# First output projection as seven half products, with all B, C and x projections ahead of the scans

## The chip, the cores and the metric

The kernel runs on one core of a Trainium2 chip. A core has five engines that run side by side, each with its own queue of instructions: TensorE (PE; its weight loads are listed as PEld), VectorE (DVE), ScalarE (ACT), GpSimd (POOL) and SyncE (SP), which issues most transfers. The metric is the device time of one execution in microseconds. A profile is taken of one execution.

## The reference

One inference step of a small trunk of two layers with width 1024. There are 1024 prompt tokens and 8 sequences of 8 new tokens, together 1088 token columns (`TOK`). Each layer is `x = x + (1 + gate) * mixer(rmsnorm(x) * (1 + scale) + shift)`, where shift, scale and gate come from a conditioning vector.

- Layer 1 is a Mamba-2 SSD mixer. One projection gives a gate z (2048 wide), x (2048), B and C (8 groups of 128 each) and dt (32 heads). x, B and C go through a causal convolution of four taps and a Silu. Then comes a scan over chunks of 128 tokens, for 8 groups of 4 heads each, with a state for each head that goes from chunk to chunk; the 64 sample tokens start from given states. The result is multiplied by silu(z), normalised over each group, and projected from 2048 back to 1024 (the output projection).
- Layer 2 is a pooling mixer: projections u and z, window means of u over 2, 4, 8 and 16 tokens, a product inside each of 4 groups, a gate, and a second output projection.
- A last norm gives y. The new convolution, scan and pool states are outputs too.

All is in fp32. Most matrix products are written as three matmuls on split numbers: a high part (fp32r) and the rest, hi*hi + hi*lo + lo*hi. Small products in the scan use plain fp32.

## The kernel before, in words

Activations lie with channels on the 128 partitions and tokens along the free axis. A tile is 128 channels by 1088 tokens. SBUF tiles of that size come from a set of 30 slots (`Slots`, 7 wide ones more in the second half). The program is written in one order, and a scheduler at build time places each instruction in its engine's queue: an instruction that is ready early may go ahead of one written before it. On the chip the queues are then in order.

Two ways of making a pair of projection tiles exist. The plain way (`mm1`, `mm3`, L179 to L187) takes three token chunks of 368, 368 and 352 (`CH`), and for each of 8 input blocks three matmuls. The fast way (`fast_run`, L1010) is a Strassen-like scheme over a pair of tiles: seven products of half the size (4 input blocks, 544 tokens as two quarters of 272), with sums of activations (`act_sums_front`, L1420, once) and of weights (`w_sums`, L939, for each pair: GpSimd makes four sums, and `split_half`, L167, splits seven half tiles into high and low parts).

Layer 1 runs like this:

- `front` (L1353) makes the norm, the first four gate tiles the plain way and dt. `front_pairs` (L1461) then makes twelve pairs the fast way, listed in `FRONT`: gates z for groups 2 to 7, and B, C and x for groups 5, 7 and 0. B, C and x tiles go through the convolution (`conv_tile`, L335), and those of groups 5 and 7 are stored in DRAM (`xbd`).
- `ssd_layer` (L1517) runs the eight scans. `scan_group` (L506) is a generator that stops after each chunk; after each stop, `FILL` says how many units of other work are written in. Those units come from `beside` (L1553): the plain projections of B, C and x for groups 1, 2, 3, 4 and 6 (one unit is one token chunk of one tile, 24 matmuls), with the blocks that make shift, scale and gate (`ada_block`, L239) between them, and then the first output projection.
- The first output projection (`op_unit`, L761) works on four parts of 4 input tiles each (`PARTS`). For each of the 8 output tiles it multiplies one part, scales by the gate and adds to x. Parts 0 to 2 are beside the scans; between the parts x goes to DRAM and back. The last part (`last_part`, L785) makes the squares and the norm of layer 2 with it, in three token chunks.

In a scan chunk `front` (L536) loads `acb`, a broadcast of the cumulative decay (two buffers), takes exponentials on ScalarE (L545, L558, L559), makes C*B and three transposes on TensorE, and products on VectorE (L561 to L577). `states` (L585) makes the chunk states, `rows` (L602) the output. At the group's end `back_sample` and `state_sample` (L637, L658) treat the sample tokens, with masked copies on ScalarE (L662) and matmuls on split numbers (L665).

Layer 2 starts with two pairs the plain way (`plain_pairs`, L871) and fourteen the fast way (`fast_pairs`, L1081). After the pooling products the second output projection already runs as seven half products: `ORDER` lists them, `block_steps` (L1154) makes the activation blocks, `ow_fetch`, `ow_add` and `ow_split` (L1184 to L1223) fetch, sum (by an accumulating DMA on GpSimd's queue) and split the weight blocks, `out_product` (L1252) multiplies, and `contribute` (L1225) adds each product to the places that need it.

## Time and profile before

| what | value |
|---|---|
| median of 3 runs | 1635.8 us (1634.3 to 1637.19) |
| the profiled execution's own time | 1634.35 us |
| its span, first to last instruction | 1632.6 us |
| TensorE busy | 1598.2 us, 98% |
| VectorE busy | 1170.1 us, 72% |
| ScalarE busy | 862.5 us, 53% |
| GpSimd busy | 443.0 us, 27% |
| from HBM, to HBM | 201.12 MB, 70.23 MB |

A row of the groups of instructions reads: line, engine, operation, what is written and read, shape and count, then busy time and the mean duration of one in ns, then the engine's idle time before them and what ended it. A duration holds the run through the engine's pipeline, so neighbours overlap and the distance of two starts is shorter. A row of a stretch gives start and end, length, busy time and number of instructions for each engine, the granted clock, the DMA share and GB/s. A row of a timeline gives the start in us and the duration.

From the trace, the stages of the execution: the twelve fast pairs from 95.9 to 358.6 us, the scan groups start at 358.6, 432.2, 507.4, 582.5, 657.9, 731.7, 809.0 and 879.9, the first output projection ends at 1000.3, the plain part of the pool projection at 1053.9, the fast part at 1353.8, the pool products at 1448.8.

### The profile page before, as it was taken

To read this page: it belongs to the slowest core of one execution; us is meant where nothing else is said; L and a number is where in the kernel's file an instruction comes from. 1 tells how busy PE (TensorE), PEld (TensorE's weight loads), DVE (VectorE), ACT (ScalarE), POOL (GpSimd) and SP (SyncE) were. 2 spreads that over 40 slices of the span, in tenths; PEclk is the share of its full clock that TensorE was granted. 3 is DMA by queue.
4 is the path that set the end of the run, shared out by engine and by line. 5 is a ranking of instruction groups with operands and counts; after the bars stand their busy time and mean duration, and the time that the engine had idled before them with its cause. 6 is when DMAs were issued, how large, how long until landed. Compare 5 with 4: busy or idle time off the path is not lost. (4 is left out here: it accounts for less than half of the span.)

```text
span 1632.6 us, 30674 instructions
## 1 busy us (share of the span) xinstructions
PE 1598.2 (98%) x12061; PEld 1521.7 (93%) x12061; DVE 1170.1 (72%) x1914; ACT 862.5 (53%) x1737; POOL 443.0 (27%) x525
## 2 busy tenths in 40 slices
PE   8999999999999999999999999999999999999997
PEld 6899999998889898888999899999999999999996
DVE  6873467568787888789878867955556547577886
ACT  6663454467667667675645536633434344333364
POOL 0233354411221202120212222354444530000241
PEclk9999999999999999999999999999999999999999
DMA  9422232354654554678889542133323369665783
GB/s 346 163 71 96 81 124 80 110 181 141 196 158 159 166 191 130 219 230 305 283 313 311 203 140 95 45 126 104 108 100 104 124 202 359 197 164 182 164 168 114
DMA packets 122305, 275.59 MB, mean 169 GB/s; under 512 B 18192, under 2 KB 59312, under 8 KB 122160
## 3 DMA queue, kind: packets, MB, share of 16 engines
q1 hardware_dynamic: 118128, 260.91, 46.8%
q0 software_dynamic: 4032, 12.72, 4.5%
q8 instruction: 95, 1.56, 0.4%
q14 instruction: 50, 0.41, 0.1%
HBM read 201.12 MB, written 70.23 MB: 166 GB/s over the span
## 5 line engine op out<-in xcount | busy, mean ns | idle before, releaser
L999 PE MATMUL st<-hh,w 128*128 128x272 f32 x832 | 240.4, 289 | 1.9 <-POOL w L175 1.9
L997 PE MATMUL st<-hh,w 128*128 128x272 f32 x832 | 240.2, 289 | 0.0
L998 PE MATMUL st<-hl,w 128*128 128x272 f32 x832 | 239.6, 288 | 0.0
L997 PE MATMUL st<-t,w 128*128 128x272 f32 x624 | 181.5, 291 | 3.9 <-DVE z L1027 2.1
L998 PE MATMUL st<-t,w 128*128 128x272 f32 x624 | 180.8, 290 | 0.7 <-DVE t L911 0.7
L999 PE MATMUL st<-t,w 128*128 128x272 f32 x624 | 181.1, 290 | 0.0
L181 PE MATMUL mm<-hh,wh 128*128 128x368 f32 (+1 forms) x528 | 178.1, 337 | 0.1
L183 PE MATMUL mm<-hh,wl 128*128 128x368 f32 (+1 forms) x528 | 173.4, 328 | 0.0
L182 PE MATMUL mm<-hl,wh 128*128 128x368 f32 (+1 forms) x528 | 173.3, 328 | 0.0
L999 PEld LDWEIGHTS st<-hh,w 128*128 128x128 f32 x832 | 156.5, 188 | 2.4 <-POOL w L175 2.4
L998 PEld LDWEIGHTS st<-hl,w 128*128 128x128 f32 x832 | 156.8, 188 | 0.0
L997 PEld LDWEIGHTS st<-hh,w 128*128 128x128 f32 x832 | 156.6, 188 | 0.1
L598 POOL TENSOR_TENSOR hd<-h,cd 128x256 f32<-128x256 f32 x56 | 49.4, 883 | 340.8 <-DVE h L599 185.2
L181 PE MATMUL mm<-gh,wh 128*128 128x368 f32 (+1 forms) x384 | 129.3, 338 | 1.6 <-ACT raw L420 1.5
L1249 PE MATMUL op<-b,w 128*128 128x272 f32 x448 | 128.9, 288 | 1.1 <-DVE b L1178 1.1
L1248 PE MATMUL op<-b,w 128*128 128x272 f32 x448 | 129.5, 289 | 0.0
L1250 PE MATMUL op<-b,w 128*128 128x272 f32 x448 | 129.0, 288 | 0.0
L182 PE MATMUL mm<-gl,wh 128*128 128x368 f32 (+1 forms) x384 | 125.9, 328 | 0.2 <-DVE gl L745 0.2
L183 PE MATMUL mm<-gh,wl 128*128 128x368 f32 (+1 forms) x384 | 126.0, 328 | 0.0
L997 PEld LDWEIGHTS st<-t,w 128*128 128x128 f32 x624 | 119.1, 191 | 4.8 <-DVE z L1027 2.3
L998 PEld LDWEIGHTS st<-t,w 128*128 128x128 f32 x624 | 118.6, 190 | 1.0 <-DVE t L911 0.9
L999 PEld LDWEIGHTS st<-t,w 128*128 128x128 f32 x624 | 118.7, 190 | 0.0
(300 smaller groups left out, 4432.7 us busy)
## 6 DMA issues: line engine op xcount, KB each, us to landing
wr<-win SPq DMA_DIRECT2D x48, 512.0 KB, 3.6
acb<-acd SPq DMA_DIRECT2D x64, 256.0 KB, 4.5
wr<-pin SPq DMA_DIRECT2D x32, 512.0 KB, 3.5
wr<-pout SPq DMA_DIRECT2D x28, 512.0 KB, 4.8
x<-x1d SPq DMA_DIRECT2D x24, 544.0 KB, 5.5
x1d<-x SPq DMA_DIRECT2D x22, 544.0 KB, 5.0
wr<-pout POOLq DMA_DIRECT2D x20, 512.0 KB, 6.1
x<-xT SPq DMA_DIRECT2D x16, 544.0 KB, 5.8
```

The costliest lines, as they stand in the source:

```text
L181: nc.tensor.matmul(ps[:, :n], hi[:, k, :], ah[:, a:a + n], start=first, stop=False)
L182: nc.tensor.matmul(ps[:, :n], hi[:, k, :], al[:, a:a + n], start=False, stop=False)
L183: nc.tensor.matmul(ps[:, :n], lo[:, k, :], ah[:, a:a + n], start=False, stop=last)
L598: nc.gpsimd.tensor_tensor(out=hd, in0=h[-1], in1=cd.unsqueeze(2).to_broadcast([P, 4, 64]), op=ALU.mult)
L997: nc.tensor.matmul(ps[c], hi[:, k], xh[:, t], start=(k == 0 and not more), stop=False, skip_group_check=True)
L998: nc.tensor.matmul(ps[c], hi[:, k], xl[:, t], start=False, stop=False, skip_group_check=True)
L999: nc.tensor.matmul(ps[c], lo[:, k], xh[:, t], start=False, stop=(k == 3), skip_group_check=True)
L1248: nc.tensor.matmul(ps[:, :QUART], hi[:, k], xh, start=k == 0, stop=False)
L1249: nc.tensor.matmul(ps[:, :QUART], hi[:, k], xl, start=False, stop=False)
L1250: nc.tensor.matmul(ps[:, :QUART], lo[:, k], xh, start=False, stop=k == 7)
```

## The change

- `FRONT` now lists sixteen fast pairs: B and C, then x, for groups 1 to 7 and then 0. All are convolved in one way; all but group 0 are stored in DRAM and read back at the end of the scan before theirs. The sixteen late ada blocks run in the front, with slots of their own for the weights.
- Beside the scans stand only the plain gate tiles of groups 2 to 7 (`gate_fill`), stored raw until both of a pair are made and then put through Silu, and then the first of the seven products of the output projection. `FILL` is 4 or 5 units a group, and 10 in the last.
- The first output projection uses the routine of the second: `out_init`, `block_steps`, `out_units`, with inputs read back from DRAM (`need_rows`) as slots allow (`room`, `reserve`). Product 2 is written beside the last scan with three accumulators, the other six after the scans (`ssd_out`).
- In the scan, the sample states are multiplied in plain fp32, half of their masks are made on VectorE, the sum of two squares is left to the ones-matmul, and a few small steps on ScalarE go.
- Layer change: the sample additions, squares, norm and modulation for the second half of the tokens are written behind products 4 and 7, those of the first half behind the first chunk of the pool projection, which now takes four token chunks of 272.
- The weight splits of the fast pairs that GpSimd did are on VectorE.

The core of the diff:

```diff
-FRONT = (("z", 2), ("z", 3), ("z", 4), ("b", 5), ("x", 5), ("z", 5), ("b", 7), ("x", 7), ("z", 6), ("b", 0), ("x", 0),
-         ("z", 7))
-BESIDE = (1, 2, 3, 4, 6)
-
-FILL = (((1,) * 10 + (2,),) * 4 + ((1,) * 9 + (4, 5),) + ((3, 2, 2, 2, 2, 2, 2, 2, 2, 2, 3),) * 2 + ((2, 2, 2, 1, 1, 1, 1, 1, 2, 2, 1),))
+FRONT = tuple((kind, g) for g in (1, 2, 3, 4, 5, 6, 7, 0) for kind in "bx")
+BESIDE = (2, 3, 4, 5, 6, 7)
+NSLOT_S = 1
+
+
...
-    def split_half(self, src, pool=False):
+    def split_half(self, src):
...
-        eng = self.nc.gpsimd if pool else self.nc.vector
-        eng.tensor_tensor(out=lo, in0=src, in1=hi.bitcast(F32), op=ALU.subtract)
+        self.nc.vector.tensor_tensor(out=lo, in0=src, in1=hi.bitcast(F32), op=ALU.subtract)
...
-            if src is None:
-                raws.append(self.stream_next_raw().rearrange("p a m -> p (a m)"))
-            else:
-                raws.append(self.slots.get("ada"))
-                nc.sync.dma_start(raws[hh][:, :1024].rearrange("p (a b) -> p a b", a=4), src[:, 4 * hh:4 * hh + 4, :])
+            raws.append(self.slots.get("ada"))
+            nc.sync.dma_start(raws[hh][:, :1024].rearrange("p (a b) -> p a b", a=4), src[:, 4 * hh:4 * hh + 4, :])
...
-        return self.gp.tile([P, 1115], F32, tag="raw", bufs=4, name=self.name("raw"))
+        return self.tp.tile([P, 1115], F32, tag="raw", bufs=5, name=self.name("raw"))
...
+    def gate_fill(self):
+
+
+        tiles = [(g, i) for g in BESIDE for i in range(2)]
+        steps = iter(())
+        for g, i in tiles:
             w = self.stream_next()
+            if i == 0:
+                dst = [self.slots.get("z") for _ in range(2)]
+            if (g, i) == tiles[-1]:
+                self.out_init(self.io["wout"], 0)
+                steps = self.half_steps()
                 ps = [self.mm_tile() for _ in CH]
                 for k in range(8):
                     for c in range(3):
                         self.mm1(ps[c], w, k, self.hn[k], CH[c], k == 0, k == 7)
                     self.slots.free(*self.hn[k])
+                    next(steps, None)
+                    if k in (1, 3, 4, 5, 6, 7):
+                        self.ow_step((k - 1) // 2 if k < 5 else k - 3)
                     if k < 7:
                         yield
                 for c in range(3):
+                    ins = self.raw_chunk(dst[i], c, ps[c])
+                for _ in steps:
+                    pass
+            else:
+                for c in range(3):
+                    ps = self.mm_tile()
+                    self.mm3(ps, w, self.hn, CH[c])
+                    ins = self.raw_chunk(dst[i], c, ps)
+                    if c < 2:
+                        yield
+            if i:
+                with self.tc.issue_after(ins.ins):
+                    for q in range(2):
+                        self.z_chunk(dst[q], dst[q], 0, TOK)
+                for q in range(2):
+                    self.gate_store(2 * g + q, dst[q])
+            yield
+
+    def ow_step(self, i):
+
+        if i < 3:
+            self.ow_fetch()
+        if 1 < i < 4:
...
-            ea = gp.tile([P, 4, 128], F32, tag="ea", bufs=3, name=self.name("ea"))
-            nc.scalar.activation(ea[:, :, :L], acb, AF.Exp)
+            ea = gp.tile([P, 4, 128], F32, tag="ea", bufs=3, name=self.name("ea")) if c else None
+            if c == 8:
+                nc.scalar.activation(ea[:, :, 0:8], acb[:, :, 7::8], AF.Exp)
+            elif c:
+                nc.scalar.activation(ea, acb, AF.Exp)
...
+                xm = gp.tile([64, 2, 256], F32, tag="xm", bufs=2, name=self.name("xs"))
+                seq = self.kc[:64, K_SEQ + 2 * b2:K_SEQ + 2 * b2 + 2]
+                if b2 % 2:
+                    for i in range(2):
+                        nc.scalar.activation(xm[:, i], xv, AF.Copy, scale=seq[:, i:i + 1])
+                else:
+                    nc.vector.tensor_tensor(out=xm, in0=xv.unsqueeze(1).to_broadcast([64, 2, 256]), in1=seq.unsqueeze(2).to_broadcast([64, 2, 256]), op=ALU.mult)
                 S = pp.tile([P, 512], F32, tag=("S", "y")[b2 % 2], bufs=1 + b2 % 2, name=self.name("S"))
                 for i in range(2):
-                    nc.tensor.matmul(S, Bt[i], xm.rearrange("p b n -> p (b n)"), start=(i == 0), stop=(i == 1))
+                    nc.tensor.matmul(S[:, 256 * i:256 * i + 256], Bt, xm[:, i], start=True, stop=True)
                 d = hsl[half][:, 512 * (b2 % 2):512 * (b2 % 2) + 512]
                 nc.vector.tensor_tensor(out=d, in0=d, in1=S, op=ALU.add)
...
+        for q in range(2):
+            for j in range(4):
+                mm = nc.tensor.matmul(ps[32 * j:32 * j + 32, :272], self.ones[:, :32], sq[q][:, 272 * j:272 * j + 272], start=q == 0, stop=q == 1,
+                                      tile_position=(0, 32 * j))
...
+        for c, ch in enumerate(((HALF, QUART), (HALF + QUART, QUART), (0, QUART), (QUART, QUART))):
             ps = [self.plain_tile(c) for _ in range(2)]
 
             for k in range(8):
                 for i in range(2):
                     self.mm1(ps[i], ws[i], k, self.hn[k], ch, k == 0, k == 7)
+            if c == 0:
+                self.first_half()
             for i in range(2):
...
+    def room(self):
+        sl = self.slots
+        return (sl.a or sl.b) and len(sl.a) + len(sl.b) + len(sl.e) > self.reserve
+
+    def need_rows(self, rows, idx):
+
+        for i in idx:
+            if i < 16 and rows[i] is None and i < self.nrows and self.room():
+                rows[i] = self.slots.get("row")
+                self.nc.sync.dma_start(rows[i], self.gyd[i])
+
     def block_steps(self, m, rows):
...
+        ada = [("G", 0, q) for q in range(4)] + [("A", 1, k) for k in range(8)] + [("G", 1, q) for q in range(4)]
+        self.ada_plan = {n: ada[max(n - 1, 0):n + 1] for n in range(0, 16, 2)}
+        self.ada_plan[15] = ada[15:]
...
+        self.rows, self.nrows, self.reserve = [None] * 16, 14, 0
+        self.fill = self.beside()
+        for _ in range(3):
+            next(self.fill)
         for g in range(8):
             sc = self.scan_group(g, T[g])
             for i, n in enumerate(FILL[g]):
                 next(sc)
+                self.reserve = (4, 2, 0, 0)[min(max(i - 6, 0), 3)]
                 for j in range(n):
                     next(self.fill)
-                    if i in (0, 3) and j == 0:
-                        next(rest, None)
+                if i in (0, 3):
+                    next(rest, None)
                 if i == 8 and g + 1 in self.G:
-                    T[g + 1] = [sl.get("xbc") for _ in range(4)]
+                    T[g + 1] = [sl.get("xbc", extra=g < 6 and j < 2) for j in range(4)]
                     for t, d in zip(T[g + 1], self.xbd[g + 1]):
                         nc.sync.dma_start(t, d)
             rest = sc
-        self.prep = self.op_part_load(3, self.acts[3])
...
+        for n in (2, 3):
+            for _ in range(n):
+                next(self.fill)
+            next(rest)
+        self.rows[14:], self.reserve = self.last_rows, 0
...
+    def beside(self):
+
+
+        yield from self.gate_fill()
+        yield from self.out_units(2, self.block_steps(6, self.rows))
 
     def ssd_out(self):
         nc, sl, x = self.nc, self.slots, self.x
+        h2 = slice(HALF, TOK)
+        for _ in range(2):
+            self.ow_fetch()
+        self.ow_add()
+        for _ in self.fill:
             pass
+        for m, nxt in ((6, 3), (3, 5), (5, 1), (1, 4)):
+            if m == 3:
+                self.load_x(range(4))
+            self.out_product(m, self.block_steps(nxt, self.rows))
+        for d in range(8):
+            self.sample_add(d)
+            nc.sync.dma_start(self.x1d[d][:, h2], x[d][:, h2])
         ss, rst = sl.get("ss"), sl.get("rst")
+        sl.free(self.sacct)
         self.hn = []
 
+        def square(d, a, first):
+            if first:
+                nc.scalar.activation(ss[:, a:a + HALF], x[d][:, a:a + HALF], AF.Square)
+                return
+            t = self.gp2.tile([P, HALF], F32, tag="mt2", bufs=self.nmt2, name=self.name("sq"))
+            nc.scalar.activation(t, x[d][:, a:a + HALF], AF.Square)
+            (nc.gpsimd if a or d > 3 else nc.vector).tensor_tensor(out=ss[:, a:a + HALF], in0=ss[:, a:a + HALF], in1=t, op=ALU.add)
+
+        def norm(a, more=()):
+            self.ms_log(ss, rst, a, QUART, 1.0 / 1024, more=list(more))
+            self.rstd(rst[:, a:a + QUART])
+
+        def modulate(k, a, n):
+            self.modulate(1, k, x[k], rst, self.hn[k][0], self.hn[k][1], a, n, x[k][:, a:a + n])
+
+        def behind4(d, c):
+            square(2 * d + c, HALF, d == c == 0)
+
+        def behind7(d, c):
+            i = 2 * d + c
+            if i == 0:
+                for _ in range(8):
+                    self.hn.append((sl.get("hh", F32R), sl.get("hl", F32R)))
+                with self.ln_set():
+                    norm(HALF)
+                    norm(HALF + QUART)
+            else:
+                modulate(i - 1, HALF, HALF)
+            if c == 0:
+                square(4 + d, 0, d == 0)
+            else:
+                square(d, 0, False)
+                nc.sync.dma_start(self.x1d[d][:, :HALF], x[d][:, :HALF])
+            if i == 4:
+                self.stream_init(self.pool_items)
+                self.stream_raw(0)
+                self.wsw = 1
+            if i == 5:
+                self.stream_raw(1)
+            if i == 6:
+                self.stream_split(0)
+                self.stream_split(1)
+                modulate(7, HALF, HALF)
+
+        self.out_product(4, self.block_steps(7, self.rows), behind4)
+        for d in range(4, 8):
+            nc.sync.dma_start(self.x1d[d][:, :HALF], x[d][:, :HALF])
+        self.out_product(7, iter(()), behind7)
+
+        def first_half():
+            with self.ln_set():
+                norm(0)
+                norm(QUART)
+            for a in (0, QUART):
                 for k in range(8):
+                    modulate(k, a, QUART)
+            sl.free(ss, rst)
+
+        self.first_half = first_half
 
     def pool_layer(self):
         nc, io, sl = self.nc, self.io, self.slots
...
```

515 lines of the change are left out of this document (177 added, 338 removed).

## The prediction

> **What bounds the kernel now.** I read the page's busy time first, then the busy time of each engine over stretches cut where the work changes, then the groups of instructions by shape, and TensorE's timeline for single prices.
>
> ```profile
> span 1632.6 us, 30674 instructions
> PE 1598.2 (98%) x12061; PEld 1521.7 (93%) x12061; DVE 1170.1 (72%) x1914; ACT 862.5 (53%) x1737; POOL 443.0 (27%) x525
> ```
>
> TensorE is busy for all but 34.4 us. So time is gained where matmuls go away, and lost where TensorE begins to wait. The stretches below are, in order: the fast projections (twelve pairs of tiles), the third scan group, the sixth and the eighth scan group, the plain part of the pool projection, and the fast part of it. Columns: start and end, length, then busy time and count for each engine, granted clock, DMA share, GB/s.
>
> ```profile
> core 0: us, PE busy (x) PEld busy (x) DVE busy (x) ACT busy (x) POOL busy (x), PEclk, DMA share, GB/s
> 95.90:358.60 262.70, 257.93 (x2037) 255.87 (x2036) 154.68 (x233) 129.30 (x252) 106.45 (x117) 0.99 0.30 102
> 507.40:582.50 75.10, 75.10 (x587) 67.44 (x588) 61.96 (x94) 51.39 (x117) 15.42 (x27) 1.00 0.53 168
> 731.70:809.00 77.30, 75.82 (x580) 68.38 (x579) 71.18 (x126) 47.77 (x108) 12.10 (x13) 1.00 0.87 285
> 879.90:938.00 58.10, 56.37 (x447) 51.68 (x446) 48.42 (x96) 31.75 (x80) 10.12 (x9) 1.00 0.69 239
> 1000.30:1053.90 53.60, 50.39 (x294) 47.95 (x293) 50.77 (x97) 35.15 (x82) 16.41 (x26) 1.00 0.15 46
> 1053.90:1353.80 299.90, 297.43 (x2354) 296.57 (x2353) 170.64 (x247) 123.66 (x261) 134.57 (x132) 0.99 0.37 129
> ```
>
> A scan group lasts 75 us and TensorE never waits in it, because 47 us of plain projection matmuls (two pairs of tiles, priced below) lie between the scan's own. VectorE is at 61.96 of 75.10 there, and at 71.18 of 77.30 in the sixth group, where TensorE idles 1.5 us. The reader is to see that the scans are covered by projection work, and that this cover is what the change takes away.
>
> **The change part by part.** Pace of the two kinds of matmul, from stretches that hold nothing else (fast pairs; pool mix; second output projection), and the count of the one that goes:
>
> ```profile
> 1090.00:1290.00 200.00, 200.00 (x1597) 200.00 (x1596) 117.47 (x167) 78.30 (x170) 92.24 (x94) 1.00 0.31 108
> 1360.00:1440.00 80.00, 80.00 (x486) 79.82 (x485) 55.66 (x77) 25.66 (x30) 3.47 (x4) 1.00 0.73 246
> 1450.00:1550.00 100.00, 100.00 (x802) 100.00 (x801) 74.17 (x138) 34.62 (x44) 13.68 (x18) 1.00 0.69 185
> L181 PE MATMUL mm<-gh,wh 128*128 128x368 f32 (+1 forms) x384 | 129.3, 338 | 1.6 <-ACT raw L420 1.5
> ```
>
> A 272-wide matmul costs 200/1597 = 125.2 ns in the fast pairs and 124.7 ns in the output products; a plain one (368, 368 and 352 wide) 80/486 = 164.6 ns. A fast pair is 7 x 2 x 4 x 3 = 168 matmuls, 21.03 us; a plain pair 144, 23.70 us.
>
> Projections: sixteen fast pairs instead of twelve, six plain pairs beside the scans instead of ten. Four pairs change kind: 4 x (21.03 - 23.70) = -10.7 us of TensorE.
>
> First output projection: 384 x 3 = 1152 plain matmuls, 189.6 us, become 7 x 4 x 2 x 8 x 3 = 1344 narrow ones, 167.6 us: -22.0 us.
>
> The first two pool tiles go from three chunks to four of 272: 144 matmuls (23.70) become 192 (23.94): +0.2 us.
>
> Inside the scans two things get dearer on TensorE. The sample states multiply in plain fp32 (two 256-wide matmuls, like L590) instead of two 512-wide split ones (L665), and the sum of squares is summed by eight matmuls instead of four.
>
> ```profile
> 882.48 0.40 PE L665 MATMUL S<-xs,Bt 128*128 128x512 f32 x1
> 882.71 0.40 PE L665 MATMUL S<-xs,Bl 128*128 128x512 f32 x1
> 883.50 0.67 PE L710 MATMUL ms<-z,ones 128*32 128x272 f32 x8
> 900.24 1.02 PE L590 MATMUL S<-xd,Bt 128*128 128x256 f32 x4
> 908.19 0.59 PE L590 MATMUL S<-xd,Bt 128*128 128x256 f32 x2
> L252 PE MATMUL am<-wr,scp 128*32 128x256 f32 x256 | 17.1, 385 | 0.0
> L261 PE MATMUL am<-kc,mp 128*128 128x9 f32 x96 | 12.5, 239 | 0.5 <-ACT mp L257 0.5
> ```
>
> Each fp32 matmul appears as two passes; two more passes cost 1.02 - 0.59 = 0.43 us, so two matmuls 0.86 us, against 2 x 0.23 = 0.46 us now (distance of the two starts): +0.40 us, 32 times, +12.8 us (at most +0.56 each, +18, if the drain in 1.02 is not overlapped). The second four sums repeat up to 0.67 us in each of 8 groups: +4.8 us (0 if they overlap wholly). An ada block costs 17.1/16 + 12.5/24 = 1.59 us; sixteen move from the scans to the front, 25.4 us, with no change of the sum.
>
> TensorE in all: -10.7 - 22.0 + 0.2 + 12.8 + 4.8 = -14.9 us. Less than half of the gain of the seven products is left.
>
> By stages: start 95.9 as before. Front: 262.70 - 12 x 21.03 = 10.3 stays, + 16 x 21.03 + 25.4 = 372.2. A scan group's own TensorE time is 75.10 - 2 x 23.70 - 3 x 1.59 = 22.9, with the dearer parts 22.9 + 1.6 + 0.6 = 25.1, eight of them 200.8. Gates 6 x 23.70 = 142.2, products 167.6, plain pool part 53.6 + 0.2, and 578.7 from there to the end. Sum 1611.2 us of span, with no idle time in the scans.
>
> What the other engines have to do in that time decides the rest. Their rows:
>
> ```profile
> L359 DVE SCALAR_TENSOR_TENSOR raw<-raw,cwh,raw 128x1112 f32<-128x1112 f32 x60 | 83.0, 1384 | 2.8 <-ACT raw L357 2.7
> L361 DVE SCALAR_TENSOR_TENSOR xbc<-raw,raw 128x1024 f32<-128x1024 f32 x20 | 24.4, 1221 | 14.6 <-ACT raw L360 14.5
> L139 DVE TENSOR_TENSOR wl<-wr,wh 128x1024 fp32r<-128x1024 f32 x49 | 60.9, 1243 | 12.6 <-ACT wh L138 9.6 <-PE st L999 2.6
> L564 DVE TENSOR_TENSOR xd<-tr,tkx 128x512 f32<-128x512 f32 x72 | 49.0, 680 | 0.0
> L357 ACT ACTIVATE raw<-raw,cwh 128x1112 f32<-128x1112 f32 x20 | 26.3, 1314 | 0.5
> L360 ACT ACTIVATE raw<-raw 128x1112 f32<-128x1112 f32 x20 | 22.5, 1125 | 4.1 <-DVE raw L359 4.1
> L420 ACT ACTIVATE raw<-mm 128x368 f32<-128x368 f32 x40 | 18.7, 471 | 13.6 <-PE mm L183 13.0
> L138 ACT ACTIVATE wh<-wr 128x1024 fp32r<-128x1024 f32 x49 | 51.6, 1053 | 48.2 <-PE mm L182 20.5 <-DMA wr<-win 9.6 <-issue 7.7
> L662 ACT ACTIVATE xs<-st,kc 128x256 fp32r<-128x256 f32 x64 | 27.8, 497 | 8.2 <-DVE st L655 7.2 <-PE S L665 1.0
> L300 ACT ACT_TABLE_LOAD x11 | 14.1, 1283 | 9.7 <-PE ms L710 9.6
> ```
>
> Scan group, VectorE: 61.96 less four convolutions (4 x (3 x 1.384 + 1.221) = 21.5) and four weight splits (5.0) is 35.5. After: + 1.9 for one and a half gate tiles' splits, + 2 x 0.68 for the masks it takes over, and about 2 less for the dropped split and sum: 37. ScalarE: 51.39 - 4 x (1.314 + 1.125 + 3 x 0.471 + 1.053) = 31.8; - 4 x 0.497 for the masks, + 3.7 for gate tiles, + 1.7 for their Silu (priced like L360), + 1.9 for table loads (two for each pair of tiles, 0.75 pairs a group): 37. TensorE: 25.1 and, from FILL, 30 units in seven groups, 4.3 x 3.95 = 17.0: 42.1 us. So TensorE stays the busiest, with VectorE and ScalarE at 88%. The nearest row to that mix is the eighth group, where VectorE is at 83% and TensorE idles 1.73 of 58.10, 3%. I take 3% of 367 us (the scans, the gates and the first product): +11 us. Bounds: 0, and the rate of the second rival below.
>
> Front, VectorE for one pair:
>
> ```profile
> L348 DVE SCALAR_TENSOR_TENSOR xbc<-raw,vec,xbc 128x1024 f32<-128x1024 f32 x36 | 53.0, 1472 | 9.4 <-ACT xbc L350 9.0
> L348 DVE SCALAR_TENSOR_TENSOR xbc<-raw,vec,xbc 128x64 f32<-128x64 f32 x36 | 15.3, 424 | 0.2
> L175 DVE TENSOR_TENSOR w<-sw,w 128x512 fp32r<-128x512 f32 x78 | 60.3, 775 | 35.5 <-ACT w L173 35.5
> L175 POOL TENSOR_TENSOR w<-wr,w 128x512 fp32r<-128x512 f32 x50 | 66.2, 1331 | 30.3 <-ACT w L173 30.3
> L1027 DVE TENSOR_TENSOR raw<-st,m 128x272 f32<-128x272 f32 x18 | 7.7, 436 | 4.4 <-PE st L999 4.1
> ```
>
> Two convolutions 6 x (1.472 + 0.424) = 11.4, seven splits 5.4 (those of POOL move to VectorE: 50 x 0.775 = 39 us, half of it in the pool part, where VectorE is at 170.64 of 299.90), about six sums 2.6: 19.4 us against 21.03 + 1.59 = 22.6 us of TensorE, 86%. I cost it at nothing; TensorE covers it.
>
> Products: the routine is that of the second output projection, where TensorE is at 100.00 of 100.00. New are fourteen row loads on SP's queue, fewer weight buffers in the first product, and POOL's accumulating DMAs, behind which the last group's hd waits in POOL's queue. +3 us for the handover, 0 to +12. Layer change: the two stretches around it idle 3.2 + 2.5 us. The second half's norm moves beside the last product, and the first half's stands behind one chunk (two tiles, 48 matmuls, 6 us); I take -3, from -5.7 to +6.
>
> 1611.2 + 11 + 3 - 3 = 1622.2 us of span. The profiled run takes 1634.35 us with its span of 1632.6, 1.75 around it, and the median of the runs is 1635.8, 0.1% above. Forecast: **1624 us**, 0.6% faster than the profiled run.
>
> **The rivals.** Scans no longer covered. The stretch with the least cover in the trace, four chunks of the last group with one short unit each:
>
> ```profile
> 897.70:915.70 18.00, 16.30 (x142) 15.18 (x141) 16.01 (x33) 10.17 (x33) 3.09 (x4) 1.00 0.93 319
> acb<-acd SPq DMA_DIRECT2D x64, 256.0 KB, 4.5
> ```
>
> 4.5 us a chunk with VectorE at 16.01 and TensorE idle 1.7. Eight chunks at that rate are 36. Of the 42.1 us of TensorE about 31 lie beside those chunks (three fill units, 11.9, and some 19 of the scan's own 25.1), 11 at the group's end. 36 + 11 = 47 instead of 42.1, +39 us over eight groups in place of +11: 1652 us. It decides from 3.4 us of idle a group. For it: acb has two buffers, and a load is issued only when ScalarE has read the one two chunks before, so two chunks cannot be quicker than landing and reading. Against: gate units can be drawn forward into the holes. [...]
>
> Full cover: no idle in the scans, 1611.2 - 3 + 1.75 = 1610 us. For it stands the third group's 75.10 of 75.10; against it 88% on two engines in place of 82% and 68%.
>
> VectorE bounds the front: five raw buffers hold five tiles of three pairs, so a late convolution holds back the sums that free the accumulators. One us for each pair, 1624 + 16 = 1640 us. It decides from 3.2 us over 19.4 a pair; 154.68 of 262.70 speaks against.
>
> Starved products: rows and blocks for want of slots, a few us at each of six handovers, about 1645 us.
>
> **How the numbers follow.** Forecast 0.52 (its own range 1612 to 1635, with 0.08 of it in the span of no change), full cover 0.08, uncovered scans 0.26, front bound by VectorE 0.08, starved products 0.06. About 0.2% is what a measurement of this kernel can tell from no change. Faster 0.44 + 0.08 = 0.52; same 0.08 + 0.02 = 0.10; slower 0.38. The range goes from full cover to just above uncovered scans, 1609 to 1656.
>
> **What would show it.** Right: pairs 21 us plus ada apart in the front, scan groups 42 to 44 us, TensorE busy some 15 us less in all, no idle in the products. Wrong: scan groups at 46 us or more with ScalarE or VectorE ending TensorE's waits; pairs at 24 us; TensorE's sum not lower, which would mean the fp32 states cost what the products save.

## The result, and the profile after

| | before | after |
|---|---|---|
| median, runs measured together (4 each) | 1635.05 us (1633.54 to 1637.19) | 1687.99 us (1681.16 to 1694.17) |
| profiled execution, its own time and span | 1634.35, 1632.6 us | 1681.16, 1679.4 us |
| ratio | | 1.0322, 95% interval 1.0273 to 1.0371 |

The kernel became 3.2% slower, where 0.6% faster was forecast; 1688 lies outside the range too. The profiled execution of the changed kernel took 0.4% less than the median, so what its stages lose is if anything too small.

The page of the changed kernel, span and busy time of the engines:

```profile
span 1679.4 us, 32000 instructions
PE 1616.2 (96%) x12527; PEld 1510.0 (90%) x12527; DVE 1260.4 (75%) x2072; ACT 888.2 (53%) x1727; POOL 455.6 (27%) x531
```

TensorE's busy time is up by 18 us, though its work was to shrink by 14.9 us; its idle time is up from 34 to 63 us. The stretches of the changed kernel, cut where the work changes (columns as before: start and end, length, busy time and count of each engine, granted clock, DMA share, GB/s). They are: the front's sixteen pairs, gates ahead of the scans, scan group 2 (four gate units beside it), group 4 (five units), group 7 up to product 2, product 2 with the end of group 7, product 6, product 3, product 1, product 4, the plain part of the pool projection, its fast part.

```profile
core 0: us, PE busy (x) PEld busy (x) DVE busy (x) ACT busy (x) POOL busy (x), PEclk, DMA share, GB/s
96.10:470.10 374.00, 366.99 (x3025) 353.43 (x3023) 293.90 (x454) 195.79 (x371) 116.21 (x185) 1.00 0.43 143
470.10:482.60 12.50, 12.50 (x80) 12.33 (x77) 9.06 (x15) 4.99 (x9) 1.44 (x2) 1.00 0.87 305
570.40:614.30 43.90, 42.53 (x351) 34.13 (x350) 33.68 (x60) 28.78 (x70) 11.17 (x11) 1.00 0.74 251
658.20:708.80 50.60, 48.40 (x376) 39.23 (x376) 42.40 (x71) 38.49 (x91) 12.41 (x13) 0.97 0.68 221
801.30:840.80 39.50, 35.15 (x270) 29.40 (x269) 30.33 (x56) 31.24 (x76) 5.22 (x7) 0.91 0.82 266
840.80:880.40 39.60, 36.38 (x276) 31.24 (x276) 34.11 (x56) 20.95 (x31) 7.99 (x7) 0.96 0.90 279
880.40:910.60 30.20, 25.77 (x195) 25.55 (x194) 23.35 (x38) 11.71 (x17) 1.75 (x2) 0.94 0.94 302
910.60:934.50 23.90, 23.90 (x194) 23.90 (x193) 17.38 (x36) 8.36 (x12) 3.48 (x4) 1.00 0.94 251
958.60:986.30 27.70, 25.76 (x195) 25.54 (x194) 20.08 (x38) 10.18 (x15) 11.47 (x13) 0.94 0.72 204
986.30:1021.10 34.80, 27.73 (x195) 26.33 (x194) 21.81 (x35) 18.17 (x25) 17.92 (x16) 0.90 0.74 167
1047.80:1098.00 50.20, 49.72 (x342) 48.89 (x341) 42.09 (x76) 31.52 (x71) 29.72 (x9) 1.00 0.19 65
1098.00:1397.80 299.80, 295.86 (x2355) 295.22 (x2353) 191.03 (x271) 124.61 (x262) 105.86 (x107) 1.00 0.36 129
```

Product 3 shows what a product costs undisturbed, 23.9 us; product 4 takes 34.8 with the same number of matmuls. The scan groups 0 to 6 take 39.6, 48.1, 43.9, 43.9, 50.5, 47.3 and 45.3 us, together 318.7.

Against the forecast (the allowance of 11 us for idle time in the scans is spread over them by their TensorE time):

| stage | forecast | measured | difference |
|---|---|---|---|
| up to the end of the front | 468.1 | 470.1 | +2.0 |
| gates ahead of the scans | 12.2 | 12.5 | +0.3 |
| scan groups 0 to 6 | 303.0 | 318.7 | +15.7 |
| group 7, last gate tile, product 2 | 62.7 | 79.1 | +16.4 |
| products 6, 3, 5, 1, 4, 7 | 146.6 | 167.4 | +20.8 |
| plain pool part | 50.8 | 50.2 | -0.6 |
| the rest | 578.7 | 581.4 | +2.7 |
| span | 1622.2 | 1679.4 | +57.2 |

The front, the layer change and the rest are as forecast. The loss lies between 482.6 and 1047.8 us, in three places of about the same size. TensorE's waits there (who waits, for what; total, times, longest, in us):

```profile
engine line waited for: us in total, times, longest us
PE S L604 <- ACT Bt L587: 10.9, 8, 4.1
PE op L1230 <- ACT b L1157: 5.2, 2, 4.4
PE op L1230 <- ACT w L1203: 4.7, 1, 4.7
PE op L1232 <- DVE w L1204: 4.3, 4, 1.9
PE S L679 <- ACT b L1157: 2.0, 1, 2.0
```

With the smaller ones they come to 33 us. TensorE's own terms for these stages are 498.7 us in the prediction, without idle time, and the stages take 565.2. So of 66.5 us above the terms 33 are shown as idle, and as much lies in time that is shown as busy.

### The profile page after: what moved, and what is told of

Same layout as the page of the kernel before. It is cut to its first block, busy times and chain, and to the rows that moved or that the text cites. A ratio compares the mean times of both kernels' runs of the same rounds, so it can differ in the third digit from the quotient of the medians.

```text
span 1679.4 us, 32000 instructions
## 1 busy us (share of the span) xinstructions
PE 1616.2 (96%) x12527; PEld 1510.0 (90%) x12527; DVE 1260.4 (75%) x2072; ACT 888.2 (53%) x1727; POOL 455.6 (27%) x531
## 5 line engine op out<-in xcount | busy, mean ns | idle before, releaser
L933 PE MATMUL st<-hh,w 128*128 128x272 f32 x960 | 278.9, 290 | 0.1
L935 PE MATMUL st<-hh,w 128*128 128x272 f32 x960 | 277.3, 289 | 1.0 <-DVE w L168 1.0
L1230 PE MATMUL op<-b,w 128*128 128x272 f32 x896 | 261.9, 292 | 10.0 <-ACT b L1157 5.2
L1232 PE MATMUL op<-b,w 128*128 128x272 f32 x896 | 261.3, 292 | 5.1 <-DVE w L1204 5.0
L1231 PE MATMUL op<-b,w 128*128 128x272 f32 x896 | 261.0, 291 | 2.2 <-DVE b L1158 2.1
L933 PE MATMUL st<-t,w 128*128 128x272 f32 x720 | 207.8, 289 | 5.3 <-ACT t L845 3.3
L935 PE MATMUL st<-t,w 128*128 128x272 f32 x720 | 207.4, 288 | 0.0
L934 PE MATMUL st<-t,w 128*128 128x272 f32 x720 | 207.1, 288 | 0.0
L933 PEld LDWEIGHTS st<-hh,w 128*128 128x128 f32 x960 | 180.8, 188 | 3.1 <-ACT mp L244 2.5
L1230 PEld LDWEIGHTS op<-b,w 128*128 128x128 f32 x896 | 171.7, 192 | 11.7 <-ACT b L1157 5.6
L935 PEld LDWEIGHTS st<-hh,w 128*128 128x128 f32 x960 | 180.6, 188 | 1.4 <-DVE w L168 1.2
L336 DVE SCALAR_TENSOR_TENSOR xbc<-raw,vec,xbc 128x1024 f32<-128x1024 f32 (+1 forms) x192 | 168.7, 902 | 17.4 <-ACT xbc L338 16.3
L1232 PEld LDWEIGHTS op<-b,w 128*128 128x128 f32 x896 | 171.3, 191 | 6.6 <-DVE w L1204 6.5
L1231 PEld LDWEIGHTS op<-b,w 128*128 128x128 f32 x896 | 171.6, 191 | 4.2 <-DVE b L1158 3.0
L933 PEld LDWEIGHTS st<-t,w 128*128 128x128 f32 x720 | 135.7, 188 | 7.4 <-ACT t L845 3.5
L168 DVE TENSOR_TENSOR w<-wr,w 128x512 fp32r<-128x512 f32 x120 | 99.4, 829 | 50.9 <-ACT w L167 50.9
L934 PEld LDWEIGHTS st<-t,w 128*128 128x128 f32 x720 | 135.2, 188 | 0.4 <-issue 0.4
L935 PEld LDWEIGHTS st<-t,w 128*128 128x128 f32 x720 | 135.5, 188 | 0.0
L174 PE MATMUL mm<-hh,wh 128*128 128x368 f32 (+1 forms) x336 | 116.5, 347 | 0.0
L175 PE MATMUL mm<-hl,wh 128*128 128x368 f32 (+1 forms) x336 | 112.9, 336 | 0.0
```

Of the source, the lines that this page charges most:

```text
L168: self.nc.vector.tensor_tensor(out=lo, in0=src, in1=hi.bitcast(F32), op=ALU.subtract)
L174: nc.tensor.matmul(ps[:, :n], hi[:, k, :], ah[:, a:a + n], start=first, stop=False)
L175: nc.tensor.matmul(ps[:, :n], hi[:, k, :], al[:, a:a + n], start=False, stop=False)
L336: nc.vector.scalar_tensor_tensor(out=d, in0=r, scalar=w[k], in1=d, op0=ALU.mult, op1=ALU.add)
L933: nc.tensor.matmul(ps[c], hi[:, k], xh[:, t], start=(k == 0 and not more), stop=False, skip_group_check=True)
L934: nc.tensor.matmul(ps[c], hi[:, k], xl[:, t], start=False, stop=False, skip_group_check=True)
```

## Experiments on the scans

The profiled runs whose edit does not touch the scans give a measure of what may be read from one profile: groups 0 to 6 take 316.5 to 321.6 us in them, group 7 with product 2 79 to 81 (74.5 with another weight buffer), product 4 34.8 to 37.2 where nothing of it was changed. Over all runs with product 2 beside the last scan and the weight sums in place, edits that aimed elsewhere moved group 7 with product 2 between 71.0 and 82.4 us, so a few us there are not to be read as the effect of one edit. Times of one kernel scatter by up to 9 us to both sides of their median.

**A third acb buffer.** The loop of two acb buffers was what the prediction named for uncovered scans.

```diff
-                t = gp.tile([P, 4, 128], F32, tag="acb", bufs=2, name=self.name("acb"))
+                t = gp.tile([P, 4, 128], F32, tag="acb", bufs=3, name=self.name("acb"))
...
```

> A third acb buffer in the scans, nothing else. Theory A (the two acb buffers hold the chunks back): a load is no longer issued behind ScalarE's reading, ScalarE's waits on acb (32 + 22 + 10 us over the eight groups in the changed kernel) go, the groups come from 45.5 to about 42 us, 1688 becomes about 1660. Theory B (the scan's own chain through VectorE and ScalarE, without enough cover, holds them): the waits on acb turn into waits on the next thing, 1688 becomes 1680 to 1688.

Measured: 1681.7 us, ratio 1.0274 (1.0252 to 1.0295). ScalarE's waits on acb over the scans, first in the changed kernel, then with three buffers:

```profile
ACT ea L565 <- DMA acb<-acd: 32.3, 22, 4.3
ACT M L578 <- DMA acb<-acd: 9.9, 6, 4.1
```

```profile
ACT ea L565 <- DMA acb<-acd: 11.0, 6, 3.8
ACT M L578 <- DMA acb<-acd: 7.3, 3, 4.3
```

The waits fall from 42 to 18 us, and the seven groups take 320.0 us in place of 318.7. So this loop alone does not hold the groups. Group 7 with product 2 was shorter (71.0 us), but that did not come back in a later run with the same buffer (79.1, see the mends below).

**Gates ahead, more cover, uneven cover.** Three kernels place the same gate units otherwise: none beside the groups 0 to 6; five beside each of the groups 0 to 5 (and more of the products beside 6 and 7); ten beside each of the groups 0 to 2 and none beside 3 to 6.

```diff
 gates ahead:
-FILL = tuple((1, 0, 0, 1, 0, 0, 1, 0, 0, 1, n) for n in (0, 1, 0, 0, 1, 0, 0)) + ...
+FILL = ((0,) * 11,) * 7 + ...
-        for _ in range(3):
+        for _ in range(33):
 more cover:
+FILL = ((1, 0, 1, 0, 1, 0, 1, 0, 0, 1, 0),) * 6 + ((1,) * 11, (1, 1, 1, 1, 1, 1, 1, 0, 0, 1, 0))
...
 uneven cover:
+FILL = ((1,) * 9 + (1, 0),) * 3 + ((0,) * 11,) * 4 + ...
```

> All gate tiles but the last are done ahead of the scans (33 units, 130 us), and the first seven scans stand bare. Theory A (with cover the gates lie in the holes of the scans): bare groups take about 36 us, VectorE's and acb's rate, so 130 + 7 x 36 = 382 us in place of 330 now: about 1740. Theory B (the gates hide almost nothing now, scans bare go at 28 us): 130 + 196 = 326, time as now, 1684 to 1690.

> The same TensorE work put beside the scans more densely: gate tiles 5 units in each of the groups 0 to 5, last gate tile and a part of product 2 beside group 6, the rest of product 2 and most of product 6 beside group 7. Theory A (a scan needs some 42 us by its own chain, as the bare groups show, and TensorE work beside it is free up to about 15 us and then adds less than its own time): groups 0 to 5 take 46 to 48 us, and the stretch from group 6 to the end of product 6 falls from 154 us to about 130: 1688 becomes 1655 to 1670. Theory B (the groups are bound by what each engine does, cover adds its full time): groups 0 to 5 rise by 3 us each, no gain: 1685 to 1695.

> The same thirty gate units, but ten beside each of the groups 0 to 2 and none beside 3 to 6. So far: 0 units 42 us (with a lower clock), 4 units 44, 5 units 48.2. Theory A (the scan's own TensorE share is 25 us where there is cover enough, as in the kernel before, and the rest are short waits that cover would fill): ten units give 39.5 + 25 = 64.5 to 66 us. Theory B (its share is 28 us however dense the cover): 68 us or more. Groups 4 to 6 about 42 us again by both.

Measured: 1773.5 us, 1.084 (1.0818 to 1.0862); 1689.1 us, 1.0342 (1.0303 to 1.038); 1727.7 us, 1.0559 (1.0530 to 1.0589). Groups 0 to 6 take 28.2 (it has no tail of another group in it), 40.0, 45.7, 41.9, 43.4, 41.6 and 44.8 us bare. Single groups, by stretches: two bare ones of the first kernel, two with five units of the second, two with ten of the third.

```profile
675.80:721.40 45.60, 36.28 (x263) 24.17 (x261) 37.52 (x66) 29.31 (x75) 11.00 (x11) 0.74 0.79 264
721.40:763.30 41.90, 33.21 (x256) 23.01 (x254) 34.17 (x66) 28.59 (x72) 11.78 (x12) 0.80 0.89 275
```

```profile
582.60:631.30 48.70, 47.69 (x375) 38.83 (x374) 38.88 (x67) 31.86 (x83) 12.71 (x13) 1.00 0.61 200
680.00:728.30 48.30, 48.30 (x376) 38.72 (x375) 37.97 (x66) 34.36 (x78) 11.73 (x14) 1.00 0.74 242
```

```profile
548.00:614.60 66.60, 64.44 (x495) 58.43 (x494) 38.28 (x68) 43.43 (x96) 11.39 (x11) 1.00 0.68 215
614.60:680.50 65.90, 64.28 (x496) 58.48 (x495) 37.77 (x67) 41.69 (x90) 13.57 (x14) 1.00 0.75 235
```

With the groups of four units of the changed kernel and the one of the kernel before, this makes a curve (a unit is 24 matmuls of 164.6 ns, 3.95 us; means over groups that have the tail of another in them):

| units beside a group | their TensorE time | group | what is left for the scan |
|---|---|---|---|
| 0 (gates ahead, groups 1 to 6) | 0 | 42.9 | 42.9 |
| 4 (changed kernel, groups 2, 3, 5, 6) | 15.8 | 45.1 | 29.3 |
| 5 (more cover, groups 1 to 5) | 19.8 | 48.2 | 28.4 |
| 10 (uneven cover, groups 1 and 2) | 39.5 | 66.3 | 26.8 |
| 12 and three ada blocks (before, group 2) | 52.2 | 75.1 | 22.9, with the dearer parts 25.1 |

Three things follow. A bare group takes about 43 us, with VectorE at 34 to 38 and the clock at 0.74 and 0.80 in the two rows: no engine is full (the busiest has 37.52 of 45.60 and 34.17 of 41.90 us), which the author takes for a chain from engine to engine. (The 36 us of the second rival were for the eight chunks alone; with the 6 us of the scan's own TensorE time that it leaves for the group's end, a bare group comes to 42 by it.) The slower clock is part of the 43: over the six groups it stands between 0.74 and 0.91, and length times (1 - clock) is 8 us a group, at most. Four units hide in that chain nearly whole, 2.2 us for 15.8, and with them the clock is at 1.00; how much of the 2.2 is owed to the clock was not separated. From there to ten units each costs (66.3 - 45.1) / 6 = 3.5 of its 3.95 us. So in the denser kernel the six groups 0 to 5 got 16 us longer and the stretch from group 6 to product 3 15 us shorter (139 in place of 154), and the time stayed: theory B in its result. The uneven kernel lies at the edge of theory A. The FILL of the change, four or five units, sits on the knee between the two sides. There the forecast took 25.1 us for the scan, a share that the kernel before shows under dense cover; with thin cover it is 28 to 29.

Where the 3 to 4 us go can be seen from the distances of starts in the timeline: in the group 570.4 to 614.3 the 96 gate matmuls take 19.5 us from each start to the next one, some 3.6 more than their pace, and 1.4 of that is shown as idle; the scan's own matmuls take 24.4, near the price of 25.1. Of the loss 2.5 us stand at the thirteen changes from a gate matmul to one of the scan: one of them takes 1.62 us, nine take 0.25 to 0.39 in place of 0.16. Whether the scan's matmul is not ready then, while the last gate matmul is still shown as busy, the trace does not tell. In the kernel before the same sum is 49.3 us for 288, 1.9 more than the pace.

**Bt first.** Most of the waits that are shown in the scans were for Bt, which ScalarE copies behind five activations of M.

```diff
+            Bt = gp.tile([P, 128], F32, tag="Bt", bufs=2, name=self.name("Bt"))
+            nc.scalar.activation(Bt[:L], pt[:L, 256:384], AF.Copy)
             M = gp.tile([P, 4, 128], F32, tag="M", bufs=3, name=self.name("M"))
...
-            Bt = gp.tile([P, 128], F32, tag="Bt", bufs=2, name=self.name("Bt"))
-            nc.scalar.activation(Bt[:L], pt[:L, 256:384], AF.Copy)
```

> In each chunk the copy of the transposed B (Bt) on ScalarE is written ahead of the five activations of M instead of behind them. Theory A (part of the 3 us of short waits in each group is TensorE waiting for Bt behind M): the waits of the state matmuls on Bt go, the seven groups fall from 318 to 305 to 312 us, 1688 becomes 1676 to 1682. Theory B (the wait goes over to M): 316 us or more, no change.

Measured: 1683.0 us, 1.0306 (1.0272 to 1.0340); the seven groups 319.8 us. TensorE's waits over them with the early copy:

```profile
PE S L604 <- ACT M L580: 4.9, 3, 4.2
PE S L679 <- DVE xs L676: 2.8, 3, 1.4
PE S L604 <- DVE xd L586: 2.3, 3, 1.1
```

The wait for Bt is gone, and the same matmul is now shown waiting for M and xd. That is theory B: here the chain handed its wait on.

**Split states.** The sample states again as in the kernel before (512-wide matmuls on split numbers, masks on ScalarE).

```diff
-                    nc.tensor.matmul(S[:, 256 * i:256 * i + 256], Bt, xm[:, i], start=True, stop=True)
+                    nc.tensor.matmul(S, Bt[i], xm.rearrange("p b n -> p (b n)"), start=(i == 0), stop=(i == 1))
...
```

> The sample states again as two 512-wide matmuls on split numbers with masks on ScalarE, as in the kernel before; all else as changed. Theory A (the plain fp32 states cost what was summed): TensorE 12.8 us less busy, and where TensorE ends the group the time falls by up to 13 us, to 1675. Theory B (the groups are held by other engines): ScalarE gains 32 masks of 0.5 us, 16 us, and the time stays or rises to 1695.

Measured: 1682.4 us, 1.0284 (1.0263 to 1.0305). The page of that run:

```profile
PE 1603.2 (96%) x12463; PEld 1496.6 (89%) x12463; DVE 1254.5 (75%) x2072; ACT 904.1 (54%) x1768; POOL 448.6 (27%) x531
```

TensorE's busy time falls by 13.0 us, where 12.8 was priced for the plain fp32 form; ScalarE's rises by 15.9. The seven groups take 312.7 us, 6 less. The price was right, and about half of it lay on the path.

## Experiments on the products

**Stores late.** In product 4 TensorE waits 4.7 us for a split weight block (L1203). The wait ends at 1012.11, ahead of the 145th of the product's 192 matmuls, so it is the last of its four blocks and not, as the expectations have it, the start of the product. The blocks of product 4 are not summed. Their split stands in ScalarE's queue behind the sign changes (L1190) of the blocks of product 7, and those wait for plain fetches, which stand on SP's queue behind stores that wait for GpSimd:

```profile
1010.06 1.06 ACT L1190 ACTIVATE wr<-wr 128x1024 f32<-128x1024 f32 x1 [2.88 <-DMA wr<-wout]
1011.02 1.04 ACT L1203 ACTIVATE w<-wr 128x1024 fp32r<-128x1024 f32 x1
```

```profile
999.96 0.33 SPq L1553 DMA_DIRECT2D x1d<-x  x1
1000.38 0.38 SPq L1175 DMA_DIRECT2D wr<-wout  x1
```

The edit writes the stores behind product 4.

```diff
             self.sample_add(d)
-            nc.sync.dma_start(self.x1d[d][:, h2], x[d][:, h2])
...
         self.out_product(4, self.block_steps(7, self.rows), behind4)
+        for d in range(8):
+            nc.sync.dma_start(self.x1d[d][:, h2], x[d][:, h2])
```

> The eight stores of the second half of x stand behind product 4 instead of ahead of its weight fetches. Theory A (the weight fetch of product 4 stood on SP's queue behind stores that wait for GpSimd): the 4.7 us gap ahead of product 4 and the slow clock behind it go, product 4 takes 25 to 28 us in place of 34.8, 1688 becomes 1677 to 1681. Theory B (GpSimd's queue itself delays the accumulating weight fetch): the gap stays, no change.

Measured: 1691.6 us, 1.0338 (1.0321 to 1.0355); product 4 35.6 us, with a wait of 4.8. But the edit did not reach the queue: the scheduler still placed a moved store (L1603) just ahead of the fetch.

```profile
998.21 0.33 SPq L1603 DMA_DIRECT2D x1d<-x  x1
998.63 0.38 SPq L1175 DMA_DIRECT2D wr<-wout  x1
```

So the run does not decide between the theories. GpSimd's timeline in the changed kernel shows what the store of 999.96 waits for, the last sample addition at 999.61, and what stands ahead of that: two runs of square sums, 4.59 and 7.11 us, with the sample addition and the accumulating fetches (L1192) between and behind them.

```profile
994.20 4.59 POOL L1564 TENSOR_TENSOR ss<-ss,sq 128x544 f32<-128x544 f32 x3
...
1000.25 0.88 POOL L1192 DMA_DIRECT2D wr<-wout  x1 [0.32 <-ACT w L1203]
1000.86 7.11 POOL L1564 TENSOR_TENSOR ss<-ss,sq 128x544 f32<-128x544 f32 x4
1007.90 0.91 POOL L1192 DMA_DIRECT2D wr<-wout  x1
```

**Squares on VectorE, no weight sums, and both.** The first puts those sums on VectorE, the second leaves the accumulating fetches of the first output projection out, the last has both, with a third acb buffer and split states.

```diff
-            (nc.gpsimd if a or d > 3 else nc.vector).tensor_tensor(out=ss[:, a:a + HALF], ...
+            nc.vector.tensor_tensor(out=ss[:, a:a + HALF], ...
 no weight sums:
-        if op:
+        if op and self.ol:
             self.nc.gpsimd.dma_start(self.owraw[n], ..., accum_op=ALU.add)
```

> The sums of the layer-2 squares behind products 4 and 7 on VectorE (0.7 us each) in place of GpSimd (1.4 to 1.9 us each). Theory A (GpSimd's queue holds the temporary tiles that the blocks share with the squares, and the accumulating weight fetches behind them): product 4 takes 25 to 28 us in place of 34.8 to 36, 1688 becomes 1676 to 1680. Theory B (the products are late for the weight sums themselves, whatever else GpSimd does): product 4 stays above 32 us.

> The weight sums of the first output projection are left out (no accumulating fetches, so the products are wrong from there on). Theory A (the accumulating fetches starve the products): all six products after the scans come to 24 to 25 us, 140.7 us from product 6 to product 7 become 122 to 125. Theory B (blocks, rows and the squares on GpSimd starve them): 132 or more stay.

> The three mends (third acb buffer, split states, squares on VectorE) and the weight sums of the first output projection left out (its products are wrong from there on). Theory A (squares on GpSimd and weight sums are together the whole loss of the products): product 4 falls to 24 to 26 us, from product 6 to product 7 it takes 120 to 124 us, and the time is 1645 to 1652, still above the kernel before: the rest is the scans. Theory B (another cause remains in the products, such as the fetches of rows or the blocks): product 4 stays at 28 us or more, 1654 or more.

| | changed kernel | squares on VectorE | no weight sums | both, with two mends |
|---|---|---|---|---|
| time, us | 1688.0 | 1682.7 | 1664.8 | 1653.8 |
| ratio to before | 1.0322 | 1.0289 (1.0246 to 1.0332) | 1.0191 (1.0140 to 1.0241) | 1.0134 (1.0099 to 1.0168) |
| group 7 to product 6 | 79.1 | 80.8 | 71.2 | 71.4 |
| product 6 | 30.2 | 30.7 | 24.7 | 26.4 |
| product 1 | 27.7 | 26.8 | 25.8 | 28.3 |
| product 4 | 34.8 | 30.6 | 29.2 | 25.7 |
| product 6 to product 7 | 140.7 | 136.1 | 127.9 | 128.3 |

Product 6 as it stands without weight sums, and product 4 with the squares on VectorE:

```profile
872.70:897.40 24.70, 24.49 (x194) 24.07 (x193) 21.04 (x35) 9.71 (x13) 0.00 (x0) 1.00 0.87 300
```

```profile
991.30:1022.00 30.70, 27.15 (x195) 25.96 (x194) 23.06 (x41) 18.95 (x26) 7.13 (x10) 0.94 0.90 199
```

Product 6 loses 5.5 us to the weight sums (3.8 between the runs with the mends), though its one long wait in the changed kernel, 4.4 us, is for an activation block (L1157) whose row had not come from DRAM:

```profile
886.26 0.72 DVE L1155 TENSOR_TENSOR bs<-row 128x544 f32<-128x544 f32 x1 [4.04 <-DMA row<-gyd]
```

Product 4 loses 4 or more to the squares on GpSimd and 5 to the weight sums, and comes to 25.7 without both. Its wait of 4.7 us is gone in each of the three runs. Group 7 with product 2 is 8 us shorter without the sums, in both pairs of runs; the third acb buffer alone came to 71.0 with the sums in place, so this part is less sure. Neither theory held alone for the first two runs. In the last one product 4 fell as theory A had it, but from product 6 to product 7 it still takes 128.3 us in place of 120 to 124. Product 1 keeps 2 to 4 us whose cause was not tried.

**Fourth weight buffer.** Are the sums late because three raw buffers keep SP's queue waiting?

```diff
-        pool, tag, bufs = (self.gp2, "sw", 2) if self.own % 5 in (1, 2) else (self.wp, "wr", 3)
+        pool, tag, bufs = (self.gs, "sx", 1) if not self.wide and n % 4 == 3 else (self.gp2, "sw", 2) if self.own % 5 in (1, 2) else (self.wp, "wr", 3)
```

> One more buffer for raw weight blocks of the output projection while the last scan runs (four instead of three). Theory A (with three buffers a weight fetch stands on SP's queue until a split has freed one, and the rows for block 6 stand behind it): the wait at the start of product 6 (4 to 5 us) goes, from the start of group 7 to product 3 it takes 96 to 102 us in place of 109, as without weight sums (96): 1688 becomes 1676 to 1681. Theory B (the accumulating fetches themselves land too late): no change, 107 us or more.

Measured: 1689.3 us, 1.0332 (1.0307 to 1.0356); group 7 to product 3 106.4 us, between the two theories, product 6 31.9 with its wait still there. No gain in time. The transfers of the changed kernel (KB each, median us from issue to landing) speak for the landing itself:

```profile
wr<-wout SPq DMA_DIRECT2D x28, 512.0 KB, 5.6
wr<-wout POOLq DMA_DIRECT2D x20, 512.0 KB, 7.6
```

Fetch and accumulation take 13.2 us one after the other before a block can be split, while TensorE uses one block in 6 us (product 3, 23.9 us for four). That this is what starves the products was argued from these rows; the runs show only that it goes away with the sums. Two things speak against the landing alone: product 5, whose blocks are summed as well, takes 24.1 us in the changed kernel, and in the second output projection the same two transfers take 5.0 and 5.9 us, 10.9 together, at full rate (TensorE busy for 100.00 of 100.00 us from 1500 to 1600).

**Product 2 after the scans.**

```diff
-... + ((1, 1, 1, 1, 1, 1, 1, 1, 0, 1, 1),)
+... + ((1, 1, 1, 1, 1, 1, 1, 1, 0, 0, 0),)
...
```

> Product 2 stands wholly behind the last scan instead of beside it; the last gate tile stays beside it. From the start of group 7 to the start of product 6 the changed kernel takes 79 us. Theory A (beside the scan the fetches of product 2, of its weights and of the rows share queues and engines with the scan, and that costs the 16 us over the forecast): the scan alone takes some 45 us and product 2 24 to 26, 69 to 72 us. Theory B (the last scan is short of cover): 46 to 50 + 24 + the start of the weights, 78 us or more.

Measured: 1694.9 us, 1.0359 (1.0329 to 1.0389); 92.0 us from group 7 to product 6. Here too the scheduler did not follow the edit wholly: 55 of the 192 matmuls of product 2 still run ahead of the scan's last one, in place of 139. Product 2 ends 78.8 us after the group's start, and then TensorE waits 13.3 us at once for the first split weight block (L1203) of product 6. The number is theory B's, but the 13.3 us are the start of the next product's weights, and the last scan alone could not be read from the run.

**Warm product 4.** Forty matmuls of no use ahead of product 4.

```diff
+        w = self.owsplit[19][0].rearrange("p k m -> p (k m)")
+        junk = self.pp.tile([P, 512], F32, tag="tr", bufs=2, name="junk")
+        for k in range(40):
+            nc.tensor.matmul(junk[:, :QUART], w[:, :P], w[:, 512:512 + QUART], start=True, stop=True)
         self.out_product(4, self.block_steps(7, self.rows), behind4)
```

> Forty more matmuls of 272 (5 us of TensorE at full pace, results unused) stand ahead of product 4, where TensorE waits 4.7 us. Theory A (the wait itself brings down the granted clock behind it): the clock of product 4 stays at 1.00, and the stretch from product 4 to product 7 falls from 34.8 to about 31 us, extra matmuls included. Theory B (the clock falls for other reasons): still 0.90, 35 us or more.

Measured: 1695.9 us, 1.0365 (1.0335 to 1.0396); product 4 34.6 us. The forty ran from 991.06 on, ahead of product 4, and the wait lies inside it, so they could not fill it: TensorE still waited 4.6 us, up to 1006.76, and the clock was 0.74 and 0.75 in the two stretches of 10 us around that. The run tells nothing on either theory.

**The mends together.** Third acb buffer, split states and squares on VectorE; then with the early Bt; then with the fourth weight buffer in place of the third acb buffer.

> The third acb buffer, the split sample states and the squares on VectorE together. If their gains add up (group 7 with product 2 8 us shorter, 6 us from the states, 4 to 5 us in product 4) the time is 1664 to 1672 us; if each mend only hands the wait to the next, 1676 to 1684.

> Third acb buffer, split states, squares on VectorE, and the early copy of Bt. If the early copy adds 6 us or more to the three mends (1665.7): 1655 to 1661. If not: 1663 to 1670.

> As four mends, but with the fourth weight buffer in place of the third acb buffer. If weight buffers hold back the stretch from group 7 to product 6: 1652 to 1658; if acb was the better use of the space: 1664 or more. Above 1645 in either case, that is, slower than the kernel before.

Measured: 1665.7 us, 1.0178 (1.0125 to 1.0232); 1666.1, 1.0188 (1.0160 to 1.0215); 1678.5, 1.0259 (1.0232 to 1.0286). The first three give some 22 us together, more than their 17 alone, though not in the stages that were expected. Product 4 comes to 30.3 us, as with its mend alone, and group 7 with product 2 stays at 79.1. The seven groups take 305.6 us, 13 less, where split states alone gave 6 and the third acb buffer nothing. The version without that buffer, with the early Bt, has them at 305.9, and with both edits they take 303.7. So either of the two edits that gave nothing alone takes some 7 us off the groups once the states are split (one profile each), as it would be if acb and Bt were links of one chain. The second of them adds nothing in time, nor does the fourth weight buffer. No version came near the kernel before; that with the weight sums left out too is still 1.3% slower.

## Why the prediction was wrong

**What bounds it.** Right that cover was what the change takes from the scans. The decision between its cases went wrong.

**TensorE's sum, -14.9 us.** Its terms held where they could be measured: fp32 states 12.8 (13.0), products 23.9 us each undisturbed (product 3), pairs and ada blocks in the front (374.0 for 372.2). But busy time rose by 18, and the text's own sign for dear fp32 states, "TensorE's sum not lower", would have misled: without them it is 1603.2, still above before. What else busy time holds was not separated; the lower clock and short waits behind a matmul that is still shown as busy are candidates.

**The scan group, 42.1 us plus 3%.** This step failed first. 25.1 us was found by subtraction from a group under dense cover, and its sum with thin cover was taken as if short waits would stay covered. The 3% came from the eighth group, which had more cover. Measured: 28 to 29 us for the scan at four to five units, 45.5 us a group on average, +15.7 us over seven. The second rival's 47 a group was nearer. Its acb loop alone was not the cause, since a third buffer gave nothing until the states were split too. Its 36 us for the eight chunks are near what the bare groups take, 38 on average up to the transposes of the sample tokens.

**VectorE and ScalarE, 37 each.** 34 to 42 and 29 to 38 in the stretches. Neither was the bound, as the text had it.

**What cover is worth.** The curve is on the side of the rival of uncovered scans: four units beside a scan cost 2.2 us in place of 15.8. It shows a limit as well, since the units from there to ten cost 3.5 of their 3.95 us each.

**Products, +3 us.** The largest miss: +20.8, and +16.4 in group 7 with product 2. The step said that the second output projection runs at 100.00 of 100.00 and let that stand for the first. The first has fewer buffers, reads its rows from DRAM, and shares GpSimd's queue with sample additions and squares; the text named GpSimd's accumulating DMAs but priced them at nothing beyond the handover. Weight sums (13 in the products, and 8 in group 7, less sure) and squares on GpSimd (some 5) are what the runs show; some 11 of the 37 us stay open, and so does how the sums do it. The fifth rival had the place and, for product 6, the late rows, at a chance of 0.06; that slots were short, as it had it, was not tried.

**The cases as alternatives.** Uncovered scans and starved products were given separate chances and separate times, 1652 and 1645. Both came at once. From 1624, their extra times are 28 and 21: together 1673, outside a range that stopped above the dearer one. That this comes within 8 us of the profiled 1681 is in part luck: the scans cost 15.7 us more than forecast, not 28, and the products with group 7 37.2, not 21.

**Front and layer change.** Right: VectorE 293.90 of 374.00 did not bound the front, and the plain pool part took 50.2 for 50.8.

**The clock.** Not in the prediction at all. The slow stretches of the table above, length times (1 - clock), come to about 14 us at most; part of that time TensorE had no work anyway, so it is not added to the rest.

## What to carry to other kernels

An engine's own time, found by subtraction where it is fully covered, holds only under that cover; with thin cover the scan's share grew here from 25 to 28 or 29 us, and part of that stood inside what is shown as busy (2.2 of 3.6 us in one group), so look at distances of starts and plan for the measured group at the cover that the change leaves. A routine that runs at full rate in one place brings its queues and buffers, not its rate, to another (here 100.00 of 100.00 us in the second output projection, and 167.4 us where 146.6 were forecast for six products of the first). Rivals that lie in different stages can come true together: their extra times add. And where a scheduler places the instructions, look in the trace whether an edit has moved them on the chip before a theory is judged by it; two of the runs here did not move what they were meant to, or only in part.

## What was not expected of the hardware

TensorE's clock fell from 1.00 to 0.50 in a wait of 4.73 us. In product 4, its timeline in the changed kernel (start, duration) around the wait for the last weight block, and the granted clock:

```profile
1006.98 0.29 PE L1231 MATMUL op<-b,w 128*128 128x272 f32 x1
1007.10 0.29 PE L1232 MATMUL op<-b,w 128*128 128x272 f32 x1
1012.11 0.59 PE L1230 MATMUL op<-b,w 128*128 128x272 f32 x1 [4.73 <-ACT w L1203]
...
1014.45 0.43 PE L1230 MATMUL op<-b,w 128*128 128x272 f32 x1
1014.67 0.43 PE L1231 MATMUL op<-b,w 128*128 128x272 f32 x1
```

```profile
995.00:1003.00 8.00, 7.69 (x62) 7.47 (x61) 4.39 (x5) 4.33 (x7) 7.37 (x8) 1.00 0.50 112
1013.00:1018.00 5.00, 4.63 (x22) 4.63 (x23) 4.99 (x9) 2.08 (x3) 0.00 (x0) 0.55 0.78 163
1018.00:1021.00 3.00, 3.00 (x26) 3.00 (x26) 0.10 (x1) 0.00 (x0) 0.00 (x0) 1.00 0.02 5
```

The starts are 0.125 us apart before the wait of 4.73 us and 0.22 behind it, for some 5 us, and the clock is back by 1018. In steps of 1 us the clock is 1.00 up to 1010, some 3 us into the wait, then 0.85, and 0.50 from 1011 to 1017. The return took about 5 us of work. A wait of 1.94 us at 977.0 was followed by a clock of 0.72 from 980 to 986, and one of 3.15 us at 732.8 by no fall (1.00 up to 744); what decides between these was not settled. In the bare scan groups 2 and 3 the clock stands at 0.74 and 0.80, with no wait of TensorE above 4.4 and 4.1 us. TensorE is shown busy there for 36.28 and 33.21 us with the scan's own work alone, where the 42.53 us of group 2 in the changed kernel leave 26.7 without their four units (15.8). So its part of the chain grew longer as cover went away, though short waits may be counted in it; how much the clock has in that was not separated.
